# A planner for one NeuronCore: when a projection group may follow its own sum, how bursts of small matmuls are formed, and how long transfers are taken to last

## The chip, the cores and the metric

One core of one Trainium2 chip runs the whole program. The time is the device time of one execution in microseconds; the table further down has the runs of the kernel before. A profile of one more execution gives the trace from which all durations here are read.

## What is computed

One step of a decoder layer with two recurrent branches: 16 meta tokens and 2048 prompt tokens, and beside them 8 sample sequences of 4 tokens. Both branches read the same normalised input through one wide projection.

```python
h = rmsnorm(x, ln1_w)
p = h @ w_in                                  # 1024 -> 10384 columns
# branch A, 8 heads of 128: short convolution + SiLU on q, k, v, then the gated delta rule by chunks of 64
t_inv = solve(eye + lower, eye)               # lower: strict triangle of k_beta k^T * decay, per chunk and head
for chunk:                                    # the state s is carried from chunk to chunk
    v_new = u - w @ s
    o     = (q * exp(gc)) @ s + qk @ v_new
    s     = s * exp(g_last) + k_tail^T @ v_new
# branch B, 16 heads of 64: RWKV-7, S = S diag(w) - (S kk)(kk*a)^T + v k^T,  y = S r
x = x + (sig(gA) * (A @ w_out_a) + sig(gB) * (B @ w_out_b)) @ w_out
y = rmsnorm(x, lnf_w)
```

## The kernel before

**Tiles and stages.** Tokens are cut into chunks of 64, and the 33 chunks into five segments of 6 or 7 chunks, so that a tile is 128 features by 384 or 448 tokens. In each segment there are four units "G" (branch A, two heads each) and eight units "R" (branch B, two heads each). A unit first has its projections (stage P), then its preparation (stage M: norms, pairwise products, transposes, the inverse of the triangle), then its chain over the chunks (stage C), in which each chunk needs the state of the chunk ahead of it. Around them stand the projections of the gates and three output projections ("f", br 0 to 2: `w_out_a`, `w_out_b`, `w_out`).

**The projections.** `proj` sums 24 matmuls of 128x128 into one PSUM tile `ps_p`: the input is held as a high and a low part (`hHL`, or `mhl` for the last projection) and so are the weights (`wh`, `wl`). Half of a tile is 12 matmuls, 8 with `wh` and 4 with `wl`; the planner keeps them as groups of six (`PG`). Each weight half is loaded from HBM by SyncE (SP) into one of ten slots with tag `w`, and SP issues all DMAs in one order.

**The small matmuls.** The chain and the preparation work on 64x64 or 128x64 pieces. The planner calls a form of the array a mode: F is 128x128 (projections, transposes, column sums), A is up to 64 by up to 64, B 128 by up to 64, C 64 by 128. In the trace they show as `128*128`, `64*64`, `128*64` and `64*128`. In the chain of a G unit the PSUM tile is `ps_g` and the tiles are `gs` (state), `gR`, `wbd`; in that of an R unit `ps_c`, `X`, `rR`, `xo`. Each chunk visits TensorE three or four times, and between two visits VectorE or ScalarE has to turn PSUM into the next operand. Such a pair of visits is called a link below.

**The inverse.** `send_blocks` and `g_inv` write the diagonal blocks to DRAM (`ex`, eight DMAs), read them back in another layout (`iM`), invert them on VectorE (`iD`, `iT`), write them (`bk`) and read them into `Dn` and `Dt` by sixteen DMAs; then TensorE multiplies out of `Dn` into `ps_n`.

**What sets the order.** Nothing runs as it was written down: `Rec` records the operations as nodes with dependences, and `Sched.run` plays through them with costs of its own (`cost`, L346; a transfer lasts `n.lat` = 2.1, L366) and appends each node to one order when it starts. `replay` (L875 in the profile) then emits that order, so each engine gets a fixed queue, and on the chip an engine waits at the head of its queue. In `run`, a node becomes ready when all it depends on has finished by the planner's clock, TensorE's own predecessors included, with 0.18 or 0.27 behind a matmul. `pick_pe` (L812) chooses TensorE's next node: it stays in a mode while that mode has ready nodes; from F it leaves for a small mode if the next projection group `pn` isn't ready, or if enough groups have run (`s.burst` counts them) and there is a link ready, or much work. `commit` (L619) lines up projection tiles and the weight loads in `worder`; `can` (L541) lets a weight load start when a slot is free, `drop` (L586) frees it.

```python
go = pn is None or (any(chain.values()) and s.burst >= BCH) or s.burst >= BMX or (val[k] >= BVL and s.burst >= BCH)
BCH, BMX, BVL, AGE, ZUR = 4, 16, 3.0, 0.1, 0.5
```

Of the kernel before, what the change touches and what calls it, by code (L numbers as in the profile page):

```python
# [16 lines left out]
C = 64  # L17
# [229 lines left out]
class Rec:  # L247
# [98 lines left out]
    def cost(s, n, e, name, a, k, outs, ins, mode):  # L346
        f = lambda x: prod(x.shape[1:])
        if e == "PE":
            n.cols += (128 if name == "transpose" else f(a[2])) * (1 if name == "transpose" or a[1].dtype == F32R else 2)
            if name == "transpose":  # L350
                n.dur += 0.107
            elif a[1].dtype == F32R:
                n.dur += (f(a[2]) / 2.4 + 14.5) / 1000
            else:
                N = f(a[2])
                n.dur += {"A": max(54, 54 + 0.5 * (N - 64)), "B": max(56, 0.86 * N), "C": max(70, 1.05 * N), "F": max(110, 4 * N / 2.4)}[mode] / 1000
            n.lat = 0.18 if a[1].dtype == F32R else 0.27
        elif e == "SP":
            o = outs[0] if outs else a[0]
            by = prod(o.shape) * 4  # L360
            last = lambda x: x.ap[-1][1] * 4 if x.ap[-1][0] == 1 else 4
            ap = [y.ap_ if isinstance(y, V) else y for y in (a[0], a[1])]
            seg = min(last(y) for y in ap)
            nd = by / max(seg, 4)
            n.kb = max(by, nd * 256)
            n.dur, n.lat = 0.07, 2.1  # L366
        else:
            N = max(f(x) for x in outs[:1] + ins[:1]) if outs else 0
            ps = any((isinstance(x, V) and x.root.psum) for x in ins)
            if e == "DVE":  # L370
                d = N / 0.96 + 160
                if name == "scalar_tensor_tensor":
                    d += 40
                if name == "tensor_tensor_scan":
                    d = 2 * N / 0.96 + 160
            elif e == "ACT":
                d = 0.82 * N + (165 if ps else 240)
            else:
                d = {"tensor_tensor": 2.35 * N + 100, "memset": 0.6 * N + 80}.get(name, 1.1 * N + 150)
            n.dur += d / 1000  # L380
            n.lat = 0.09
        if e == "PE":
            return
# [63 lines left out]
class Sched:  # L447
# [4 lines left out]
    def __init__(s, rec, porder):  # L452
# [42 lines left out]
        for u in rec.units:  # L495
            ev = []
            for j, n in enumerate(u.nodes):
                for r in n.allocs:
                    r.left = len(r.acc)
                    r.unit = u  # L500
                    k = (r.pool, r.tag)
                    if r.psum or r.tag == "w":
                        continue
                    u.seqs.setdefault(k, []).append(r)
            last = {}
            for j, n in enumerate(u.nodes):
                for r in n.roots:
                    last[r] = j
            start = {r: j for j, n in enumerate(u.nodes) for r in n.allocs}
            for k, L in u.seqs.items():  # L510
                live = []
                for i, r in enumerate(L):
                    live.append(1 + sum(1 for q in L[:i] if last[q] >= start[r] or q.unit is not u or any(m.unit is not u for m in q.acc)))
                mx = 0
                pk = [0] * (len(L) + 1)
                for i in range(len(L) - 1, -1, -1):
                    mx = max(mx, live[i])
                    pk[i] = mx
                u.peak[k], u.idx[k], u.held[k] = pk, 0, 0
                if mx > rec.slots[k]:  # L520
                    print("PEAK", u.kind, u.seg, k[1], mx, rec.slots[k])
            u.left = len(u.nodes)
            for n in u.nodes:
                u.st.setdefault(n.stage, [0, []])
                u.st[n.stage][0] += 1
                u.st[n.stage][1].append(n)
# [14 lines left out]
    def can(s, n):  # L541
        need = {}
        for r in n.allocs:
            k = (r.pool, r.tag)
            need[k] = need.get(k, 0) + 1
        u = n.unit
        for k, c in need.items():
# [1 line left out]
            if av < 0:  # L549
                return False  # L550
            if k[1] == "w":
                if not s.worder or s.worder[0] is not n:
                    return False
                continue
            if k[0].space == PSUM:
# [30 lines left out]
    def drop(s, r):  # L586
        k = (r.pool, r.tag)
        s.free[k].append(r.slot)
        if k in r.unit.held and not r.psum and r.tag != "w":
            r.unit.held[k] -= 1  # L590

# [108 lines left out]
    def run(s):  # L700
# [2 lines left out]
        E = ["PE", "DVE", "ACT", "POOL", "SP"]  # L703
        s.rdy = {e: [] for e in E}
        s.active, s.worder, s.pq, s.cur, s.infl, s.wpend = [], [], [], None, [], []
        s.lastunit, s.late = s.porder["last"], s.porder["late"]
        tfree = dict.fromkeys(E, 0.0)
        s.mode, s.burst = "F", 0
# [3 lines left out]
        ev, c = [], 0  # L712
# [8 lines left out]
        while done < total:  # L721
            s.commit()
            prog = True
            while prog:
                prog = False
                for e in E:
# [7 lines left out]
                    if e == "PE":  # L734
# [9 lines left out]
                            s.cols[w] = s.cols.get(w, 0) + n.cols * part / d  # L744
                        s.mode = n.mode
                        isP = n.pt is not None and len(n.ops) * 2 > PG
                        s.burst = s.burst + 1 if isP else (s.burst if n.mode == "F" else 0)
                        s.stat["P" if isP else "s"] += n.dur
                        s.stat["idle"] += s.now - max(tfree[e], 0)
# [3 lines left out]
                        s.rdy[e].remove(n)  # L753
                    s.take(n)
                    n.started, n.start = True, s.now
                    s.on_started(n)
                    out.append(n)
                    nstart += 1
# [8 lines left out]
                    heapq.heappush(ev, (fin, c, n))  # L767
                    if e == "PE":
                        s.commit()
            if not ev:  # L770
                self_dump(s)
                raise RuntimeError("stuck")
# [5 lines left out]
            for n in L:  # L778
                if n is None:
                    continue  # L780
                done += 1
                n.unit.left -= 1
                if n.unit.left == 0:
                    s.active.remove(n.unit)
                for r in n.roots:
                    r.left -= 1
                    if r.left == 0:
                        s.drop(r)
                for m in n.succ:
                    m.nd -= 1  # L790
                    m.rt = s.now
                    if m.nd == 0 and m.en and not (m.pt is not None and m.eng == "PE"):
                        s.rdy[m.eng].append(m)
        s.order = out
        return out

    def clock(s):
        w = int(s.now / 3.4133)
# [13 lines left out]
    def pick_pe(s):  # L812
# [10 lines left out]
        else:  # L823
# [8 lines left out]
            T = {k: L for k, L in R.items() if k != "F"}  # L832
            if T:
                val = {k: sum(x.dur + (0.5 if x.cls == 0 else 0.0) for x in L) + AGE * max(s.now - x.rt for x in L) for k, L in T.items()}
                chain = {k: any(x.cls == 0 for x in L) for k, L in T.items()}
                k = max(T, key=lambda k: (val[k], k))
                go = pn is None or (any(chain.values()) and s.burst >= BCH) or s.burst >= BMX or (val[k] >= BVL and s.burst >= BCH)
                if go:
                    n = min(T[k], key=key)
            if n is None and "F" in R:  # L840
# [19 lines left out]
                    print("       ", r.name, "next", L[i].name, i, len(L), "free", len(s.free[k]), "peak", u.peak[k][i], [(v.age, v.held.get(k), v.peak[k][v.idx[k]] if k in v.idx else None) for v in s.active])  # L860


BCH, BMX, BVL, AGE, ZUR = 4, 16, 3.0, 0.1, 0.5


def replay(tc, rec, order):
# [1446 lines left out]
```

## Time and profile before

| what | us |
| --- | --- |
| runs | 4485.87, 4490.87, 4494.15; median 4490.87 |
| the profiled execution's own time | 4488.34 |
| its span, first to last instruction | 4486.6 |
| VectorE, ScalarE, GpSimd busy | 2725.4, 1973.8, 984.4 |
| read from HBM, written | 602.29 MB, 180.56 MB |

The profile groups instructions by source line and tile names; as `replay` emits everything, one line stands for all, and the tile names tell the work. "Idle before" is the time for which an engine had nothing running ahead of an instruction, with the instruction or DMA that ended it. Single-precision matmuls that aren't of the rounded kind stand as two records each, so a chain step of two matmuls shows as x4.

### The profile page before, as it was taken

How to read it: one execution, taken by the hardware profiler on the slowest of the kernel's cores; microseconds unless marked ns; L12 is line 12 of the kernel's file. 1: busy time of each engine (PE TensorE's matmuls, PEld its weight loads, DVE VectorE, ACT ScalarE, POOL GpSimd, SP SyncE). 2: the span in 40 equal slices, each digit the busy share in tenths (PEclk: the TensorE clock that was granted, in tenths of full speed). 3: DMA queues.
4: the chain of work that ended last, by engine and by line, in shares of the span. 5: the costliest groups of instructions: out<-in, count | busy, mean ns of one | idle time of the engine just before them, and what ended most of it. 6: DMA issues, size and time to landing. Idle time of an engine off the chain costs nothing. (4 is left out here: it accounts for less than half of the span.)

```text
span 4486.6 us, 91248 instructions
## 1 busy us (share of the span) xinstructions
PE 4138.6 (92%) x32684; PEld 3467.9 (77%) x32684; DVE 2725.4 (61%) x7052; ACT 1973.8 (44%) x4842; POOL 984.4 (22%) x1972
## 2 busy tenths in 40 slices
PE   6788999998999999998999999999999999989997
PEld 6677777777878788877777787878777888768776
DVE  5877766756666554556667544676654547656642
ACT  5444543434445344444444442545444434544431
POOL 3333333323122121112212121121122102211210
PEclk9887898899999899999999999999999999999998
DMA  7544665659645456754445576544446865444457
GB/s 253 179 139 139 194 222 173 193 192 306 189 130 164 126 175 214 248 175 121 138 125 150 166 238 212 178 127 144 135 135 183 258 192 174 137 122 131 142 181 241
DMA packets 660687, 790.08 MB, mean 176 GB/s; under 512 B 251105, under 2 KB 347209, under 8 KB 660234
## 3 DMA queue, kind: packets, MB, share of 16 engines
q1 hardware_dynamic: 660234, 784.25, 56.5%
q8 instruction: 259, 4.24, 0.4%
q14 instruction: 194, 1.59, 0.1%
HBM read 602.29 MB, written 180.56 MB: 174 GB/s over the span
## 5 line engine op out<-in xcount | busy, mean ns | idle before, releaser
L875 PE MATMUL ps_p<-hHL,wh 128*128 128x448 f32 (+3 forms) x7760 | 1938.3, 378 | 39.2 <-DMA wh<-wh 20.3
L875 PEld LDWEIGHTS ps_p<-hHL,wh 128*128 128x128 f32 x7760 | 1395.4, 195 | 186.6 <-issue 62.7
L875 PE MATMUL ps_p<-hHL,wl 128*128 128x448 f32 (+3 forms) x3880 | 910.1, 357 | 1.5 <-DVE wl L875 1.0
L875 PEld LDWEIGHTS ps_p<-hHL,wl 128*128 128x128 f32 x3880 | 727.8, 193 | 36.8 <-DVE wl L875 1.6
L875 POOL COPY xo<-X 64x64 f32<-64x64 f32 x528 | 177.4, 336 | 819.5 <-ACT X L875 445.2
L875 DVE TENSOR_TENSOR iT<-iM,iD 56x1 f32<-56x1 f32 (+1 forms) x900 | 293.2, 326 | 72.4 <-DMA iD<-in_consts 54.7
L875 ACT COPY raw<-ps_p 128x448 f32<-128x448 f32 (+3 forms) x285 | 144.0, 505 | 341.2 <-PE ps_p L875 316.2
L875 DVE SCALAR_TENSOR_TENSOR cv<-raw,pv,cv 128x448 f32<-128x448 f32 (+1 forms) x360 | 261.1, 725 | 37.0 <-ACT cv L875 28.1
L875 DVE TENSOR_REDUCE iD<-iT 56x1 f32<-56x1 f32 (+1 forms) x900 | 205.1, 228 | 17.6
L875 POOL TENSOR_TENSOR wl<-wr,wh 128x512 fp32r<-128x512 f32 x105 | 146.4, 1394 | 218.7 <-ACT wh L875 101.9
L875 ACT ACTIVATE X<-ps_c,dc 64x64 f32<-64x64 f32 x224 | 69.0, 309 | 266.7 <-DVE X L875 153.4
L875 ACT CAST wh<-wr 128x512 fp32r<-128x512 f32 x210 | 129.3, 616 | 114.5 <-PE ps_p L875 36.2
L875 ACT ACTIVATE X<-ps_c 64x64 f32<-64x64 f32 x264 | 54.3, 216 | 261.7 <-DVE X L875 134.9
L875 DVE SCALAR_TENSOR_TENSOR gs<-gs,gl,ps_g 128x128 f32<-128x128 f32 x264 | 84.5, 344 | 125.2 <-PE ps_g L875 86.8
L875 POOL TENSOR_TENSOR Nt<-AL,consts 64x448 f32<-64x448 f32 (+1 forms) x80 | 93.7, 1171 | 292.9 <-DVE AL L875 288.4
L875 PE MATMUL ps_p<-mhl,wh 128*128 128x448 f32 (+2 forms) x640 | 156.1, 371 | 0.6 <-DMA wh<-wh 0.4
L875 ACT ACTIVATE sig<-cv 128x448 f32<-128x448 f32 (+2 forms) x120 | 67.4, 561 | 185.6 <-DVE cv L875 184.3
L875 PE MATMUL ps_g<-gs,cv 128*64 128x128 f32 x1056 | 122.1, 307 | 25.7 <-DVE wbd L875 9.6
L875 DVE TENSOR_SCALAR X<-ps_c,dc 64x64 f32<-64x64 f32 x224 | 65.1, 291 | 128.2 <-PE ps_c L875 83.8
L875 PEld LDWEIGHTS ps_n<-Z,Wp 64*64 64x64 f32 x3168 | 113.2, 146 | 34.5 <-DVE Z L875 15.4
L875 PE MATMUL ps_n<-Z,Wp 64*64 64x16 f32 (+1 forms) x3168 | 123.1, 222 | 12.4 <-DVE Z L875 12.1
L875 DVE TENSOR_TENSOR Z<-Dt,ps_n 128x336 f32<-128x336 f32 (+1 forms) x180 | 67.0, 372 | 101.7 <-PE ps_n L875 84.2
(337 smaller groups left out, 7483.4 us busy)
## 6 DMA issues: line engine op xcount, KB each, us to landing
wh<-wh SPq DMA_DIRECT2D x1050, 256.0 KB
wl<-wl SPq DMA_DIRECT2D x1050, 256.0 KB
wr<-in_wt SPq DMA_DIRECT2D x210, 256.0 KB
gl<-gt SPq DMA_DIRECT2D x72, 224.0 KB
gt<-gt SPq DMA_DIRECT2D x48, 224.0 KB
xt<-in_x_prompt SPq DMA_DIRECT2D x29, 256.0 KB
xt<-in_x_prompt SPq DMA_DIRECT2D x13, 512.0 KB
out_y_p<-xt SPq DMA_DIRECT2D x26, 256.0 KB
```

The source lines that it names most:

```text
L875: getattr(getattr(nc, eng), name)(*[g(x) for x in a], **{q: g(x) for q, x in k.items()})
```

## The change

Six edits, all in the planner; no operation is added or left out, and both orders have 23653 matmuls.

1. A node of TensorE that depends on another node of TensorE counts that one as done when it starts (`settle`, called at the start), not when it ends plus 0.18 or 0.27. A group that goes on with its own sum, and any other matmul behind TensorE's own work, may go at once.
2. Leaving F for a link: it is no longer enough that one unit's link is ready and four groups have run. There must be links of as many units as have a chain begun and unfinished (`na`), or one that has been ready for 3.0 (`TWAIT`).
3. Out of a small mode, the next small mode with ready nodes is taken, not the projections (`DIR`).
4. `BCH`, `BMX`, `BVL` go from 4, 16, 3.0 to 2, 8, 1.5.
5. Transfers other than weight loads are taken to last 3.0 in place of 2.1 (`DLAT`).
6. A weight slot is not reused for 1.0 after it was freed (`WMAR`), by the planner's clock.

```diff
-            n.dur, n.lat = 0.07, 2.1
+            n.dur, n.lat = 0.07, WLAT if n.stage == "W" else DLAT
...
+            k = sum(1 for n in u.nodes if n.eng == "PE" and n.stage == "C" and n.mode in "AB")
+            u.chain = [k, k]
...
-                if not s.worder or s.worder[0] is not n:
+                if not s.worder or s.worder[0] is not n or (WMAR and s.freed.get(s.free[k][0], 0) > s.now - WMAR):
...
+                    if e == "PE":
+                        for m in n.succ:
+                            if m.eng == e:
+                                s.settle(m)
...
                 for m in n.succ:
-                    m.nd -= 1
-                    m.rt = s.now
-                    if m.nd == 0 and m.en and not (m.pt is not None and m.eng == "PE"):
-                        s.rdy[m.eng].append(m)
+                    if m.eng != n.eng or m.eng != "PE":
+                        s.settle(m)
...
-                chain = {k: any(x.cls == 0 for x in L) for k, L in T.items()}
+                na = sum(1 for u in s.infl if 0 < u.chain[0] < u.chain[1])
+                chain = {}
+                for k, L in T.items():
+                    C = [x for x in L if x.cls == 0]
+                    chain[k] = bool(C) and (len({x.unit for x in C}) >= na or max(s.now - x.rt for x in C) >= TWAIT)
...
-                go = pn is None or (any(chain.values()) and s.burst >= BCH) or s.burst >= BMX or (val[k] >= BVL and s.burst >= BCH)
+                go = pn is None or (s.mode != "F" and val[k] >= DIR) or (any(chain.values()) and s.burst >= BCH) or s.burst >= BMX or (val[k] >= BVL and s.burst >= BCH)
...
-BCH, BMX, BVL, AGE, ZUR = 4, 16, 3.0, 0.1, 0.5
+BCH, BMX, BVL, AGE, ZUR = 2, 8, 1.5, 0.1, 0.5
+WLAT, DLAT, WMAR = 2.1, 3.0, 1.0
+DIR = 0.0
+TWAIT = 3.0
```

Two places show what becomes of TensorE's order. The first is the end of the chain of the last R unit, in the last segment: the column sums over `sh` and `sl` (high and low part) are its last visits to TensorE, and behind them stand the projections. Before:

```order
L875 MATMUL ps_p<-hHL,wh 128x448 x2
L875 MATMUL ps_p<-hHL,wl 128x448 x4
L875 MATMUL ps_a<-consts,rs_277 64x64 x2
L875 MATMUL ps_p<-hHL,wh 128x448 x6
L875 MATMUL ps_n<-sh,bocm 128x448
L875 MATMUL ps_n<-sl,bocm 128x448
L875 MATMUL ps_p<-hHL,wh 128x448 x2
L875 MATMUL ps_p<-hHL,wl 128x448 x4
L875 MATMUL ps_a<-sh,bocm 128x448
L875 MATMUL ps_a<-sl,bocm 128x448
L875 MATMUL ps_p<-hHL,wh 128x448 x8
```

The same place of the order now:

```order
L903 MATMUL ps_p<-hHL,wh 128x448 x8
L903 MATMUL ps_p<-hHL,wl 128x448 x4
L903 MATMUL ps_n<-sh,bocm 128x448
L903 MATMUL ps_n<-sl,bocm 128x448
L903 MATMUL ps_a<-consts,rs_277 64x64 x2
L903 MATMUL ps_p<-hHL,wh 128x448 x8
L903 MATMUL ps_p<-hHL,wl 128x448 x4
L903 MATMUL ps_a<-sh,bocm 128x448
L903 MATMUL ps_a<-sl,bocm 128x448
L903 MATMUL ps_p<-hHL,wh 128x448 x8
```

Twelve projection matmuls now stand between two visits of the chain where six stood. Of the projections behind the last row of `sl`, up to the first that reads `mhl`, there were 192, which are the eight tiles of the second output projection; now there are 324, so 132 matmuls of earlier work have moved behind the chain's end and ahead of the first matmul that needs its result.

The second place is a G unit in the fourth segment, where TensorE first multiplies out of `Dn`, with the chains of another G unit (`ps_g`) and an R unit (`ps_c`) around it. Before:

```order
L875 MATMUL ps_p<-hHL,wh 128x448 x2
L875 MATMUL ps_p<-hHL,wl 128x448 x4
L875 MATMUL ps_p<-hHL,wh 128x448 x6
L875 MATMUL ps_g<-gR,Z 64x128 x2
L875 MATMUL ps_c<-rR,Z 64x64 x2
L875 MATMUL ps_n<-Dn,Nt 64x64 x14
L875 MATMUL ps_p<-hHL,wh 128x448 x2
L875 MATMUL ps_p<-hHL,wl 128x448 x4
```

The same unit in the order now:

```order
L903 MATMUL ps_p<-hHL,wh 128x448 x6
L903 MATMUL ps_g<-gR,Z 64x128 x2
L903 MATMUL ps_n<-Dn,Nt 64x64 x14
L903 MATMUL ps_c<-X,AL 64x64 x2
L903 MATMUL ps_g<-gs_264,cv 64x128
L903 MATMUL ps_g<-wbd_259,KE 64x128
L903 MATMUL ps_g<-gs_265,cv 64x128
L903 MATMUL ps_g<-wbd_259,KE 64x128
L903 MATMUL ps_g<-wbd_259,ktl 128x256
L903 MATMUL ps_p<-hHL,wh 128x448 x2
```

The burst now goes from the 64x64 form straight to the 128x64 form and holds the next step of both chains; between `gR,Z` and the step behind it on the same unit there is no projection matmul any more. And between this unit's pairwise product and `Dn` there are now 140 projection matmuls where there were 96.

More of the change, by code (lines that the diff above doesn't have):

```diff
@@ L588, in drop @@
         s.free[k].append(r.slot)
+        if r.tag == "w":
+            s.freed[r.slot] = s.now
+            if WMAR:
+                s.wake.append(s.now + WMAR + 0.001)
         if k in r.unit.held and not r.psum and r.tag != "w":
@@ L705, in run @@
         s.active, s.worder, s.pq, s.cur, s.infl, s.wpend = [], [], [], None, [], []
+        s.freed, s.wake = {}, []
         s.lastunit, s.late = s.porder["last"], s.porder["late"]
@@ L746, in run @@
                         isP = n.pt is not None and len(n.ops) * 2 > PG
+                        if n.stage == "C" and n.mode in "AB":
+                            n.unit.chain[0] -= 1
                         s.burst = s.burst + 1 if isP else (s.burst if n.mode == "F" else 0)
@@ L769, in run @@
                         s.commit()
+            for x in s.wake:
+                c += 1
+                heapq.heappush(ev, (x, c, None))
+            s.wake = []
             if not ev:
@@ L789, in run, with settle @@
                 for m in n.succ:
-                    m.nd -= 1
-                    m.rt = s.now
-                    if m.nd == 0 and m.en and not (m.pt is not None and m.eng == "PE"):
-                        s.rdy[m.eng].append(m)
+                    if m.eng != n.eng or m.eng != "PE":
+                        s.settle(m)
         s.order = out
         return out
+    def settle(s, m):
+        m.nd -= 1
+        m.rt = s.now
+        if m.nd == 0 and m.en and not (m.pt is not None and m.eng == "PE"):
+            s.rdy[m.eng].append(m)
     def clock(s):
```

## The prediction

> **What bounds the kernel now.** I read the page first, then the clock, then the waits of TensorE, then stretches of its timeline.
>
> ```profile
> span 4486.6 us, 91248 instructions
> ...
> PE 4138.6 (92%) x32684; PEld 3467.9 (77%) x32684; DVE 2725.4 (61%) x7052; ACT 1973.8 (44%) x4842; POOL 984.4 (22%) x1972
> ```
>
> TensorE is busy for 92% and no other engine for over 61%, so the kernel is bound by TensorE. But "busy" holds three things that are no work: the time lost when the array changes its form, the time at half clock, and, in the other 8%, waits. The planner can touch only these three, since both orders hold the same 23653 matmuls.
>
> ```profile
> core 0: 4486.6 us, clock 0.936
> ```
>
> The clock row gives the second: single stretches of the timeline run at full or at half speed, so a mean of 0.936 says that 2 x 6.4% = 13% of the span, some 574 us, ran at half. By stretches, the first 1000 us are much worse than the rest:
>
> ```profile
> 0.00:1000.00 1000.00, 874.32 (x6912) 725.65 (x6913) 691.54 (x1865) 459.06 (x1142) 325.71 (x620) 0.86 0.59 187
> 1000.00:4487.00 3487.00, 3264.23 (x25774) 2742.22 (x25772) 2033.82 (x5187) 1514.78 (x3701) 658.66 (x1352) 0.96 0.56 173
> ```
>
> The third is in the table of who waited for whom (us in total, times, longest):
>
> ```profile
> PE ps_c L875 <- DVE X L875: 39.6, 28, 6.5
> PE ps_n L875 <- DMA Dn<-bk: 34.1, 23, 5.7
> PE ps_p L875 <- DMA wh<-wh: 20.7, 4, 16.6
> ...
> PE ps_c L875 <- DVE rR L875: 16.7, 17, 4.0
> PE ps_g L875 <- DVE gR L875: 16.3, 16, 5.4
> PE ps_c L875 <- ACT X L875: 15.1, 17, 3.0
> ...
> PE ps_n L875 <- DMA Dt<-bk: 7.3, 5, 2.6
> ```
>
> The waits are many and short; the largest single one is 16.6 us. The rows of `X`, `rR` and `gR` are links of the chains (87.7 us in 78 waits, 1.12 each), those of `Dn` and `Dt` the inverse's way through DRAM.
>
> **Term 1, changes of form.** What does a visit to a small form cost? First a stretch of projections without any, then one visit, then one change inside a burst:
>
> ```profile
> 3504.43 1.76 PE L875 MATMUL ps_p<-hHL,wh 128*128 128x448 f32 x8
> 3506.03 0.96 PE L875 MATMUL ps_p<-hHL,wl 128*128 128x448 f32 x4
> 3506.83 1.76 PE L875 MATMUL ps_p<-hHL,wh 128*128 128x448 f32 x8
> ```
>
> ```profile
> 4358.59 1.48 PE L875 MATMUL ps_p<-hHL,wh 128*128 128x448 f32 x6
> 4360.00 0.33 PE L875 MATMUL ps_c<-rR,Z 64*64 64x64 f32 x4
> 4360.26 0.68 PE L875 MATMUL ps_p<-hHL,wh 128*128 128x448 f32 x2
> ```
>
> ```profile
> 3280.33 0.34 PE L875 MATMUL ps_c<-RH,xo 128*64 128x64 f32 x4
> 3280.45 0.34 PE L875 MATMUL ps_c<-AY,X 128*64 128x64 f32 x4
> 3280.71 0.99 PE L875 MATMUL ps_n<-Z,Wp 64*64 64x16 f32 x28
> ```
>
> Twelve projection matmuls take 3506.83 - 3504.43 = 2.40 us, 0.20 each. Four small records take 3280.45 - 3280.33 = 0.12. Both starting points of the visit stand just behind a return: 4360.26 - 4358.59 = 1.67, less 6 x 0.20 and less 0.12, leaves 0.35 us for leaving and coming back. Inside a burst the change costs 3280.71 - 3280.45 - 0.12 = 0.14.
>
> Counted by the forms of the matmuls, the order of before leaves the 128x128 form 1196 times, the new one 893 times; changes among small forms go from 258 to 647 (2650 and 2433 changes in all). So 303 visits fewer x 0.35 = -106 and 389 changes more x 0.14 = +54: **-52 us**. Upper end: nothing, since a visit from a transpose rather than a projection may be cheaper than the one I priced; lower end -106, if changes inside a burst hide behind each other.
>
> The Trainium skill, page "TensorEngine Tiling (Array Packing)", section "Key Properties", says that a change of the tiling mode drains TensorE, and speaks of no cheaper change between two small modes, which is against going from mode to mode. By it each change costs alike, half a visit, and the term would be 217 x 0.175 = -38. The rows have 0.14 against 0.175, so the rule is nearly right and the sum barely moves.
>
> **Term 2, the end of the last chain.** The wait of 16.6 us stands at the first place of the order shown above, and the chain of waits says what it was made of:
>
> ```profile
> 4376.16 0.47 PE L875 MATMUL ps_a<-sl,bocm 128*128 128x448 f32 x1 [0.93 <-DVE sl L875]
> 4393.25 3.33 PE L875 MATMUL ps_p<-hHL,wh 128*128 128x448 f32 x8 [16.61 <-DMA wh<-wh]
> ```
>
> ```profile
> 4380.55 0.38 SPq L875
> ...
> 4383.44 4.94 DMA hHL<-oB
> 4388.39 4.72 DMA wh<-wh
> ```
>
> The last unit's result is stored at about 4380, SP issues the eight loads of it into `hHL`, and behind them, in SP's queue, the weights. Now 132 matmuls x 0.20 = 26.4 us of projections stand behind the chain's end, which covers the 4 us to the store, and in SP's new order the weights of five halves stand ahead of the loads. What is late next: the loads overwrite the tiles that the first output projection reads, so they start only when its last tile is nearly done. A load takes 4.94, I allow 1 for its split into high and low part, and four of the eight may start some 3 us early. I take 5 us of wait as left (ends 0 and 16.6): **-12 us**.
>
> **Term 3, Dn and Dt.** The rows above hold 41.4 us. The planner counted an issue on SP as 0.07; SP needs
>
> ```profile
> L875 SPq DMA_DIRECT2D Dn<-bk x480: 302/427/1750, 161.5 to 4290.7; - x160
> ```
>
> so the eight loads of `Dn` and eight of `Dt` come 16 x 0.36 = 5.7 us later than planned, and `DLAT` gives back 0.9 in each of four transfers in a row, 3.6. Eight of the 60 units account for most of these waits. In their orders, the projection matmuls between pairwise product and `Dn` go from 140, 126, 138, 156, 132, 138, 96 and 126 to 196, 168, 162, 182, 184, 144, 140 and 184: 38 more on average, 7.7 us, against a longest wait of 5.7. Over all 60 the median goes from 132 to 147. I take three quarters of the 41.4: **-30 us** (ends 0, if SP's queue makes the loads later by as much, and -41).
>
> **Term 4, links.** I put the waits of the chains into classes by how many projection matmuls the order has between the two visits. Before, of 162 links with none, 66 waited, 0.29 us per link over all 162; of 468 with up to six, 0.115; of 286 with seven to twelve, 0.026; of 220 with more, 0.021. The new order has 281, 25, 633 and 197 of them: 81 + 3 + 17 + 4 = 105 against 113 us. **-7 us**. The two parts pull against each other: twelve matmuls between links in place of six cover nearly every link, but bursts that hold two steps of one chain make 119 more links without cover. Ends: -50, if the 119 stand behind other small work, as `gR,Z` does behind 14 matmuls of `Dn` in the order; +126 is the slower rival's.
>
> **Term 5, the clock behind a wait.** A wait costs more than itself. At the second place of the order:
>
> ```profile
> 3028.57 0.44 PE L875 MATMUL ps_n<-Dn,Nt 64*64 64x64 f32 x2 [2.32 <-DMA Dn<-bk]
> 3030.18 1.75 PE L875 MATMUL ps_n<-Dn,Nt 64*64 64x64 f32 x26 [1.16 <-DMA Dn<-bk]
> 3031.86 1.11 PE L875 MATMUL ps_p<-hHL,wh 128*128 128x448 f32 x2
> 3032.77 1.70 PE L875 MATMUL ps_p<-hHL,wl 128*128 128x448 f32 x4
> 3034.40 0.70 PE L875 MATMUL ps_g<-gs,cv 128*64 128x128 f32 x4
> ...
> 1988.65 1.00 PE L875 MATMUL ps_n<-Dn,Nt 64*64 64x64 f32 x26 [1.21 <-DMA Dn<-bk]
> 1989.58 0.67 PE L875 MATMUL ps_p<-hHL,wh 128*128 128x448 f32 x2
> ```
>
> The 26 records take 3031.86 - 3030.18 = 1.68 against 0.93 at full clock, the six projections behind them 2.54 against 1.20: 2.1 us on top of the 3.5 us waited. Eight such units: **-17 us** (ends 0 and -34).
>
> How long must a wait be for this? Here one of 2.35 us was enough, six projections taking 2.20 behind it (up to the next start) and 1.13 ahead of it:
>
> ```profile
> 1602.76 1.20 PE L875 MATMUL ps_p<-hHL,wh 128*128 128x384 f32 x6
> 1603.89 0.34 PE L875 MATMUL ps_c<-X,AL 128*64 128x64 f32 x4
> ...
> 1607.83 0.74 PE L875 MATMUL ps_a<-consts,xt 128*128 128x128 f32 x4 [2.35 <-issue]
> 1608.21 2.27 PE L875 MATMUL ps_p<-hHL,wh 128*128 128x384 f32 x6
> 1610.41 0.48 PE L875 MATMUL ps_c<-rR,Z 64*64 64x64 f32 x4
> ```
>
> The Trainium skill, page "TensorE: Matmul & The Clock Gate", section "HAM oscillation — how this bites in real kernels", has the abstract rule that idle gaps over about 3.4 us must be avoided. By it most of the waits here, which are shorter, would cost no clock, and term 5 would fall away; this trace disagrees, with its 2.35 us.
>
> **What costs nothing, I hold.** The later reuse of a weight slot (`WMAR`) delays loads by up to 1.0 by the planner's clock; what hides it is that weights come early: besides the 16.6 us, the row `wh` above holds three waits of 4.1 us in all. If that cover went, I would expect those to double, +4. Longer bursts could by themselves lack the matmul columns that keep the clock up; the bursts that hold over 2.5 us of work by the rows' durations go from 20 to 50, but none of the trace's half-clock rows that I read began without a wait, so I count 0.
>
> Not seen by any of this is where the new order meets the chip badly: each order has its own spots where the plan was too hopeful, and I removed only those of the old one. I add back a third of terms 2, 3 and 5: **+20 us**.
>
> **Sum.** 4488.34 (the profiled execution) - 52 - 12 - 30 - 7 - 17 + 20 = 4390. The median of the runs lies 2.5 us above the profiled execution, so 4393.
>
> **Rivals.**
> - *The waits only move.* For: the Dn waits are a plan's error of some us, and such errors are as likely in a new order; terms 2 to 5 give nothing. Against: 38 more matmuls ahead of `Dn`, and 132 behind the last chain. Only the changes of form stay: 4488 - 52 + 2.5 = 4439.
> - *Short waits cost no clock*, as the rule on the gate would have it. Then removing waits under 3.4 us brings only themselves: 4393 + 17 = 4410. The 2.35 us row speaks against it.
> - *Waits fall everywhere.* Edit 1 makes the plan truer, and with `DLAT` all 41 us of Dn and Dt go, half of the links' 113, and in the first 1000 us the clock rises from 0.86 half way to 0.96, 50 us: 4488 - 52 - 17 - 41 - 56 - 17 - 50 + 2.5 = 4258; with half of the excess over my sum, 4325.
> - *Slower: bursts become the place to wait.* The 119 more links without cover each wait the mean of the chain rows, 1.12 us: +133; every fourth also loses the clock, 30 x 2.1 = +63. In place of -7 that gives 4393 + 7 + 196 = 4596. For: uncovered links had the dearest class. Against: only 66 of 162 waited. It decides from (98 - 7 + 9) / 119 = 0.84 us per link, where the time would be slower by 0.2%.
> - *Within 0.2%*, about what a measurement of this kernel can tell from no change: the links take back just what the rest gives, 0.7 to 0.8 us each. That the change does nothing is excluded by the order.
>
> **Chances.** Forecast 0.50; waits only move 0.18; waits fall everywhere 0.13; short waits cost no clock 0.04; within 0.2% 0.06; slower 0.09. Faster by over 0.2%: 0.50 + 0.18 + 0.13 + 0.04 = 0.85. The range goes from 4315, which takes in most of the wide gain, to 4465, which takes in the moved waits.
>
> **What would show it.** Right: TensorE's busy time falls by some 50 to 70 us; the row `Dn<-bk` under 12 us and `Dt` near 0; at the end one wait of about 5 us on `hHL` in place of 16.6; clock about 0.945; rows of `X`, `rR` and `gR` together near 80. Wrong: a clock at or under 0.936, rows of `ps_c` and `ps_g` that hold over 200 us (the slower rival), or a `Dn` row as long as before (SP's queue). If busy time falls by 50 and idle time not at all, the waits have moved.

## The result, and the profile after

| | before | now |
| --- | --- | --- |
| median of the runs, us | 4488.37 (4482.38 to 4494.15, 4 runs) | **4363.57** (4352.51 to 4371.86, 4 runs) |
| ratio, with its 95% interval | | 0.9721 (0.9695 to 0.9746) |
| the profiled execution, and its span | 4488.34; 4486.6 | 4371.86; 4370.1 |

The kernel is 125 us faster. The forecast was 4393, so the gain came out 29 us larger than its sum. The first lines of the profile's page for the changed kernel, and its clock row:

```profile
span 4370.1 us, 91290 instructions
...
PE 4066.9 (93%) x32684; PEld 3485.0 (80%) x32684; DVE 2726.3 (62%) x7052; ACT 1965.2 (45%) x4842; POOL 992.3 (23%) x1972
```

```profile
core 0: 4370.1 us, clock 0.941
```

TensorE is busy for 4138.6 - 4066.9 = 71.7 us less with the same number of matmuls, and idle for 348.0 - 303.2 = 44.8 us less. The other engines do what they did. The two stretches of the prediction again (their columns: length, busy time and count of PE, PEld, DVE, ACT, POOL, then PE's clock, the DMA share and GB/s):

```profile
0.00:1000.00 1000.00, 867.00 (x6959) 730.75 (x6960) 707.13 (x1872) 466.93 (x1151) 333.29 (x624) 0.86 0.59 189
1000.00:4371.00 3371.00, 3199.92 (x25726) 2754.28 (x25725) 2019.17 (x5181) 1498.31 (x3691) 659.01 (x1348) 0.96 0.58 178
```

The first 1000 us run at 0.86 as before, and hold only 47 more of the 32684 records; nearly all of the gain lies behind them. Who TensorE waited for, in the rows that answer to those of before (us in total, times, longest):

```profile
PE ps_c L903 <- DVE X L903: 26.9, 22, 4.3
PE ps_c L903 <- DVE rR L903: 26.0, 20, 5.2
...
PE ps_g L903 <- DVE gR L903: 11.4, 5, 5.1
PE ps_c L903 <- ACT X L903: 10.7, 20, 1.4
...
PE ps_n L903 <- DMA Dt<-bk: 8.4, 6, 2.6
...
PE ps_n L903 <- DMA Dn<-bk: 4.5, 7, 1.1
...
PE ps_p L903 <- DMA wh<-wh: 2.0, 2, 1.0
```

`Dn` and `Dt` fell from 41.4 to 12.9 us. All rows of `ps_c` and `ps_g`, the chains, fell from 121.9 to 97.4. The 16.6 us on `wh` are gone. All waits of the table together went from 331.4 to 289.4 (without the row of `ps_a` that names no releaser, 2.4 us before).

To see where the span went, the same sum was made over the trace of every kernel: from each matmul record's start to the next start, less the median distance of that kind behind its own kind at full clock. What is over goes into three heaps: under 0.7 us at full clock (changes of form, above all), 0.7 us or more at any clock (stalls), and under 0.7 us at a lower clock.

| us | span | forms | stalls | half clock |
| --- | --- | --- | --- | --- |
| before | 4486.6 | 393 | 295 | 233 |
| now | 4370.1 | 321 | 266 | 204 |
| difference | -116.5 | -73 | -29 | -29 |

What is left, +15 us, is in the medians themselves and at both ends.

The heaps are an estimate. The heap of forms also holds waits of under 0.7 us, and its size hangs on what is taken as a kind: with kinds by both tile names and shape it falls from 586 to 532, with kinds by PSUM tile and shape from 514 to 443. (With kinds by shape alone, which mix different work, it rises from 475 to 526, as the medians themselves shift.) Stalls and half clock fall in the first two recounts as well, by 35 and by 25 to 32.

### The profile page after: what moved, and what is told of

It reads as the page before. It is cut to its first block, busy times and chain, and to the rows that moved or that the text cites. A ratio compares the mean times of both kernels' runs of the same rounds, so it can differ in the third digit from the quotient of the medians.

```text
span 4370.1 us, 91290 instructions
## 1 busy us (share of the span) xinstructions
PE 4066.9 (93%) x32684; PEld 3485.0 (80%) x32684; DVE 2726.3 (62%) x7052; ACT 1965.2 (45%) x4842; POOL 992.3 (23%) x1972
## 5 line engine op out<-in xcount | busy, mean ns | idle before, releaser
L903 PE MATMUL ps_p<-hHL,wh 128*128 128x448 f32 (+3 forms) x7760 | 1828.1, 373 | 30.7 <-ACT wh L903 10.3
L903 PEld LDWEIGHTS ps_p<-hHL,wh 128*128 128x128 f32 x7760 | 1421.3, 195 | 156.1 <-issue 28.3
L903 PE MATMUL ps_p<-mhl,wh 128*128 128x448 f32 (+2 forms) x640 | 141.5, 359 | 5.7 <-ACT wh L903 4.5
L903 DVE TENSOR_SCALAR X<-ps_c 64x64 f32<-64x64 f32 x264 | 58.8, 227 | 131.1 <-PE ps_c L903 88.9
L903 PE MATMUL ps_a<-RH,LH 64*128 64x128 f32 x1056 | 129.3, 292 | 0.0
```

What stands on the lines that cost most here:

```text
L903: getattr(getattr(nc, eng), name)(*[g(x) for x in a], **{q: g(x) for q, x in k.items()})
```

## The experiments

Twelve kernels ran. In some expectations, and below, visits are the leavings of the 128x128 form in the planner's own order, counted by its nodes: 1139 before and 839 now, with 253 and 639 changes inside bursts (the prediction's 1196 and 893 count the finished program by matmuls). "Links" are the chain's, by the projection matmuls between two visits: none, up to 6, up to 12, more. Ratios are to the kernel before as it ran beside each (medians of 4488 to 4494), with 95% intervals; the clock, and the waits of TensorE for `Dn` and `Dt` and in its chain rows (`ps_c`, `ps_g`), are from one profiled execution each.

| run | what differs | median, us | ratio | clock | Dn, Dt | chains |
| --- | --- | --- | --- | --- | --- | --- |
| before | | 4488.37 | 1 | 0.936 | 41.4 | 121.9 |
| now | all six edits | 4363.57 | 0.9721 (0.9695 to 0.9746) | 0.941 | 12.9 | 97.4 |
| e1 | without edit 1 | 4425.83 | 0.9851 (0.9826 to 0.9875) | 0.952 | 32.7 | 102.9 |
| e2 | without edit 5 | 4339.99 | 0.9661 (0.9647 to 0.9675) | 0.949 | 17.6 | 104.5 |
| e3 | now, reshuffled | 4344.03 | 0.9673 (0.965 to 0.9697) | 0.943 | 7.9 | 104.1 |
| e4 | before, reshuffled | 4523.91 | 1.0078 (1.0058 to 1.0097) | 0.934 | 45.4 | 134.1 |
| e5 | before, edit 1 alone | 4880.23 | 1.0877 (1.084 to 1.0915) | 0.872 | 47.7 | 272.3 |
| e6 | without edit 4 | 4546.79 | 1.0131 (1.01 to 1.0161) | 0.915 | 18.1 | 190.5 |
| e7 | before, transfers 3.2 | 4429.75 | 0.9871 (0.9842 to 0.99) | 0.945 | 13.7 | 115.6 |
| e8 | now, SP's issue 0.42 | 4246.63 | 0.9468 (0.9439 to 0.9497) | 0.957 | 2.6 | 86.4 |
| e9 | before, SP's issue 0.42 | 4298.55 | 0.9576 (0.9544 to 0.9608) | 0.956 | 13.2 | 52.1 |
| e10 | e8, reshuffled | 4236.65 | 0.9443 (0.9408 to 0.9477) | 0.958 | 4.1 | 67.4 |
| e11 | without edit 3 | 4505.05 | 1.0032 (1.001 to 1.0055) | 0.924 | 6.2 | 148.2 |
| e12 | edit 6 nearly undone | 4323.78 | 0.9633 (0.9596 to 0.9671) | 0.952 | 11.4 | 101.1 |

### How much is the luck of an order? (e3, e4)

`AGE` weighs the age of a waiting node by a tenth; 0.11 changes ties and near-ties all over the program and no rule. e3 is the changed kernel with it, e4 the kernel before.

```diff
-BCH, BMX, BVL, AGE, ZUR = 2, 8, 1.5, 0.1, 0.5
+BCH, BMX, BVL, AGE, ZUR = 2, 8, 1.5, 0.11, 0.5
```

> A control: the changed planner with AGE at 0.11 in place of 0.10, which has no meaning for the chip but gives another order (855 visits, 649 inside; 287, 22, 666 and 161 links with none, up to six, up to twelve and more projection matmuls as cover). Theory: 16 visits and 10 changes more are 7 us: 4371, and what any new order moves by chance is under 20 us. Rival (the gain of the change is a lucky order): over 30 us away from 4364, towards 4488.

> The same control on the kernel before: AGE at 0.11 (1154 visits, 247 inside, before 1139 and 253). Theory: 5 us more by changes of form, 4490 within 20. Rival (an unlucky order before): over 30 us below 4488.

A reshuffle without meaning moved the one by -20 and the other by +36 us. e3 came out 27 below its 4371 and e4 34 above its 4490, both more than the 20 that the theory allowed, and neither as its rival has it. So no edit that moves the time by less than some 35 us can be judged by its time alone; with two reshuffles this is a rough size. And the gain itself is no luck of the order: 4344 against 4524 is more than 4364 against 4488. The wait at the end of the last chain, which term 2 counted as removed, came back in e3:

```profile
PE ps_p L903 <- DMA wh<-wh: 21.4, 5, 16.6
```

It has its 16.6 us with all six edits in force, and its order has 192 projection matmuls behind the chain's end, as before, not 324. That the wait is gone in the changed kernel is luck of the order.

### Edit 1, taken out and put in alone (e1, e5)

e1 is the changed kernel in which a node again counts as done for TensorE only at its planned end:

```diff
-                    if e == "PE":
-                        for m in n.succ:
-                            if m.eng == e:
-                                s.settle(m)
...
-                    if m.eng != n.eng or m.eng != "PE":
-                        s.settle(m)
+                    s.settle(m)
```

> The changed planner without its first edit: a matmul node that depends on TensorE's own work counts it as done when it ends plus 0.18 or 0.27, as before; all other edits stay. Its order leaves the 128x128 form for a small one 1075 times (before 1139, changed 839, counted by the same tally) and changes 536 times between small forms (253, 639). Theory (changes of form carry the gain, 0.35 us a visit and 0.14 us inside a burst): 236 visits more x 0.35 less 103 x 0.14 is 68 us more than the changed kernel, 4430, and some 20 us more for links, since 548 of them have six projection matmuls as cover: 4430 to 4450. Rival (the longer transfers and the weight margin carry it, edits 5 and 6): within 15 us of the changed kernel, 4350 to 4380.

Measured 4425.83: 62 us over the changed kernel, 4 us below what the theory said. The forms heap is 418 us in place of 321, so the saving in forms hangs on edit 1. The clock is higher without it, 0.952, so in this pair part of the saving is paid back there: (1 - 0.952) x 4421.4 = 212 us were lost to it, against 258 in the changed kernel. And the wait for `Dn` is back, with transfers still counted as 3.0:

```profile
PE ps_n L898 <- DMA Dn<-bk: 24.8, 20, 4.0
...
PE ps_n L898 <- DMA Dt<-bk: 7.9, 11, 1.6
```

e5 is the reverse: the kernel before with these same lines the other way round, and nothing else.

> The kernel before with the first edit alone (a matmul node may follow TensorE's own work at once), thresholds and all else as before. Its order changes form least of all so far: 695 visits to small forms and 657 changes among them (before 1139 and 253). But 764 links of the chains have no projection matmul as cover (before 162, changed 281). From the runs so far a visit is worth 0.5 us, a change inside 0.2, a link without cover 0.25 to 0.29. Theory (edit 1 only pays together with the smaller thresholds of edit 4, because bursts of 16 groups starve the chains): -222 + 81 for forms, +100 for links, and some 80 for the clock behind those waits: 4490 + 40 = 4530, not under 4450. Rival (edit 1 alone carries the gain): 4490 - 141 = 4350.

Slower was right, but 390 us in place of some 40. The page of e5, its clock row, and the largest of its waits:

```profile
PE 4284.3 (87%) x32684; PEld 3650.5 (75%) x32684; DVE 2745.2 (56%) x7052; ACT 1980.5 (40%) x4842; POOL 988.6 (20%) x1972
```

```profile
core 0: 4898.7 us, clock 0.872
```

```profile
PE ps_c L883 <- ACT X L883: 82.3, 104, 7.3
```

Its order leaves 128x128 only 695 times and has the smallest forms heap of all, 265 us. But of its 1136 links 764 have no projection between them, and they waited 0.35 us each. The chain rows hold 272.3 us, and what the clock lacks of full speed went from 6.4% to 12.8%. Fewer changes of form, bought with uncovered links, is the slower rival of the prediction in full.

### Edits 4 and 3, taken out (e6, e11)

e6 has the old thresholds:

```diff
-BCH, BMX, BVL, AGE, ZUR = 2, 8, 1.5, 0.1, 0.5
+BCH, BMX, BVL, AGE, ZUR = 4, 16, 3.0, 0.1, 0.5
```

> The changed planner with its fourth edit undone: BCH, BMX, BVL at 4, 16, 3.0 again. 611 visits, 796 changes inside (changed 839, 639); 666 links without cover (281). Theory (smaller thresholds keep the chains moving): forms -114 + 31, links +92, clock behind them +74: 4364 + 83 = 4447, and the wait rows of ps_c and ps_g go from 97 to near 190 us. Rival (only changes of form count): 4364 - 83 = 4280.

The theory's mechanism holds: 666 uncovered links at 0.28 us, and chain rows of 190.5 us as expected. The time was 100 us above its number. For the clock behind the waits it had counted 74 us; (1 - 0.915) x 4550.5 = 387 against 258 is 129. For forms it had counted -83; in the first two recounts the heap of forms falls by 36 and 25 only.

e11 takes out the rule that goes from one small mode to the next:

```diff
-DIR = 0.0
+DIR = 1e9
```

> The changed kernel without edit 3: out of a small mode the planner may go back to the projections. Its order leaves 128x128 975 times in place of 839, has 396 changes among small forms in place of 639, and 390 links without cover in place of 281. Theory (a visit costs 0.35, a change inside 0.14, an uncovered link 0.25): +48 - 34 + 27 = +41, so 4405, 4380 to 4430 with the luck of the order; the chain rows near 125 us. Rival (going from mode to mode brings nothing, as visits and changes trade evenly): 4345 to 4375, chain rows near 97.

4505.05, 141 us above the changed kernel and 0.3% slower than the one before. The direction is the theory's, the size again not: 390 links without cover cost 0.30 each, and the chain rows hold 148.2 in place of the expected 125.

```profile
PE ps_c L903 <- ACT X L903: 43.2, 49, 5.2
```

```profile
core 0: 4520.1 us, clock 0.924
```

The clock is most of what the theory left out. The time lost at half speed is what the clock lacks of full speed times the span: (1 - 0.941) x 4370.1 = 258 us in the changed kernel, (1 - 0.924) x 4520.1 = 344 here, 86 more. The profiled execution is 17 us above the median, though; at 0.931, the median clock of the ten runs, it is some 53 more.

### Edits 5 and 6, taken out (e2, e12)

```diff
-WLAT, DLAT, WMAR = 2.1, 3.0, 1.0
+WLAT, DLAT, WMAR = 2.1, 2.1, 1.0
```

> The changed planner with its fifth edit undone: transfers last 2.1 again. Changes of form stay (836 visits, 635 inside). The projection matmuls between pairwise product and Dn fall from a median of 147 back to 132, and 15 units have under 120 (changed 7, before 18). Theory: the waits for Dn and Dt come back to 30 to 40 us from 12.9 and bring 10 to 17 us at half clock: 4364 + 27 + 14 = 4405. Rival (Dn was covered by the larger bursts, not by the counted length): rows of Dn and Dt under 20 us, time 4355 to 4375.

The theory fell. With transfers counted as 2.1 again the time is 24 us lower, within the luck of the order, and these are its rows:

```profile
PE ps_n L903 <- DMA Dn<-bk: 12.4, 15, 2.0
...
PE ps_n L903 <- DMA Dt<-bk: 5.2, 5, 1.5
```

17.6 us, not 30 to 40. So in the new order it isn't `DLAT` that keeps `Dn` from being late. What `DLAT` does show on is VectorE, whose wait for `iM`, the step ahead of `Dn`, is 105.1 us in e2 against 69.8 in the changed kernel and 135.3 before.

e12 counts the margin for a freed weight slot as 0.1:

```diff
-WLAT, DLAT, WMAR = 2.1, 3.0, 1.0
+WLAT, DLAT, WMAR = 2.1, 3.0, 0.1
```

> The changed kernel with edit 6 nearly undone: a weight slot may be used again 0.1 after it was freed, in place of 1.0. Its order has 842 visits and 620 changes inside (839 and 639). Theory (the later reuse is hidden, weights come early): no more than the luck of the order, 4335 to 4390, and waits on wh within 10 us of the 10 to 20 of the changed kernel. Rival (the margin protects against weights that come late): waits on wh of over 40 us and 4400 or more.

4323.78 is 11 us below what the theory allowed for, and waits on `wh` are 0.9 us against 2.0. (The expectation's "10 to 20" for `wh` was misread from the rows: 14.7 us stand there for weights that ScalarE makes, 2.0 for the load.) The margin protects against nothing that can be seen; whether it costs some of those 40 us, or the order was lucky, is not settled.

### Longer transfers in the old planner (e7)

```diff
-            n.dur, n.lat = 0.07, 2.1
+            n.dur, n.lat = 0.07, 2.1 if n.stage == "W" else 3.2
```

> The kernel before with transfers other than weights counted as 3.2 in place of 2.1 and nothing else (3.0 alone ends in a plan that gets stuck). Forms as before (1167 visits, 244 inside). Projection matmuls between pairwise product and Dn: median 148, 11 units under 120 (before 132 and 18; changed 147 and 7). Theory as predicted (the cover in matmuls decides): rows of Dn and Dt fall from 41 to under 20 us, time 4490 - 21 - 12 = 4457. Rival (pace: as long as the planner puts 0.18 us between the groups of a sum that the chip doesn't need, projections on the chip run ahead of the plan and every transfer comes late): rows of Dn and Dt stay at 30 or more, time within 30 us of 4490.

By itself, edit 5's idea is worth 59 us on the old planner and takes `Dn` and `Dt` from 41.4 to 13.7. With a visit count of 1167 the forms stay (406 us), as they should. In the changed kernel it brings nothing of that, as e2 shows.

### What an issue on SyncE costs (e8, e9, e10)

The planner counts a DMA's issue as 0.07 us of SP's time. Here is a place of the kernel before that the prediction's Dn rows come from, SP's queue first, then VectorE, then TensorE (start, duration; what ended the idle time ahead in brackets):

```profile
3025.22 3.73 SPq L875 DMA_DIRECT2D Dn<-bk  x8
3029.00 3.73 SPq L875 DMA_DIRECT2D Dt<-bk  x8
3032.77 0.42 SPq L875 DMA_DIRECT2D iD<-in_consts  x1
3033.29 0.34 SPq L875 DMA_DIRECT2D wh<-wh  x1
3033.72 0.38 SPq L875 DMA_DIRECT2D wl<-wl  x1
3034.15 0.41 SPq L875 DMA_DIRECT2D iM<-ex  x1
```

```profile
3026.40 0.22 DVE L875 TENSOR_SCALAR X<-ps_c 64x64 f32<-64x64 f32 x1
3037.03 0.29 DVE L875 TENSOR_SCALAR iM<-iM 56x256 f32<-56x256 f32 x1 [10.41 <-DMA iM<-ex]
...
3037.54 0.29 DVE L875 TENSOR_SCALAR X<-ps_c,dc 64x64 f32<-64x64 f32 x1
...
3038.04 0.35 DVE L875 SCALAR_TENSOR_TENSOR gs<-gs,gl,ps_g 128x128 f32<-128x128 f32 x1
```

```profile
3039.12 0.44 PE L875 MATMUL ps_g<-gs,cv 128*64 128x128 f32 x4 [1.45 <-DVE gs L875]
```

The sixteen loads of `Dn` and `Dt` keep SP busy from 3025.22 to 3032.77, 7.55 us where the plan has 16 x 0.07 = 1.1. Behind them stands another unit's `iM`. VectorE has it at the head of its queue and stands still for 10.41 us, and behind it stand the next `X` and `gs` of two chains; TensorE then waits 1.45 us for `gs`. So a load that nobody on TensorE waits for holds up the chains. e8 is the changed kernel, e9 the kernel before, with a count that agrees with these rows:

```diff
-            n.dur, n.lat = 0.07, 2.1
+            n.dur, n.lat = 0.42, 2.1
```

> The changed planner with SP's issue of a transfer counted as 0.42 in place of 0.07, near the 0.43 that the trace has for the loads of Dn. 866 visits, 639 inside; 312 links without cover; Dn median 168, 4 units under 120. Theory (VectorE's waits for iM and TensorE's for Dn are off the path by now): VectorE's wait for iM falls from 70 to under 40 us, Dn and Dt under 8, but the time moves by less than 20 us from 4364, +14 for forms and +8 for links. Rival (late transfers still hold the chains up through VectorE's queue): 4320 or less.

> The kernel before, with nothing changed but the planner's count of a DMA issue on SyncE (0.42 in place of 0.07). Its order leaves 128x128 about as often as before (1163 and 1154 to 1167 in the two other variants of the old planner), so forms bring nothing. Theory: the price of the issue works by itself, through VectorE's queue: VectorE's wait for iM falls from 135 to 20 to 40 us, Dn and Dt from 41 to under 10, the first 1000 us rise from a clock of 0.86 to about 0.91, and the time is 4350 to 4400, at least 30 below the 4430 that longer transfers alone gave. Rival (the price only pays where bursts hold several chains, since only there a stalled VectorE holds more than one of them): iM and Dn fall, but the time stays at 4420 to 4460.

> The changed kernel with the issue on SyncE counted as 0.42, as in the run of 4247, and AGE 0.11 in place of 0.1, which only reshuffles the order. Theory (late transfers were the cause of the gain): 4220 to 4280, iM under 40 us, Dn and Dt together under 8. Rival (the 4247 was a lucky order): back towards 4340, with a clock near 0.943.

For e8 my theory was wrong by 100 us and the rival right: 4246.63. Its rows fell as the theory had them (VectorE's wait for `iM` to 21.4 us, `Dn` and `Dt` to 2.6), but they were not off the path. The reshuffled e10, 4236.65, shows that it wasn't luck. And e9, **one number in the old planner, gives 4298.55**, 65 us faster than the six edits under study. Its clock, TensorE's waits, and VectorE's for `iM` in e9 and, below it, in the kernel before:

```profile
core 0: 4296.0 us, clock 0.956
```

```profile
PE ps_c L875 <- DVE rR L875: 12.7, 16, 1.6
...
PE ps_n L875 <- DMA Dn<-bk: 9.8, 12, 2.3
...
PE ps_c L875 <- DVE X L875: 8.3, 17, 1.5
PE ps_c L875 <- ACT X L875: 8.2, 19, 1.0
```

```profile
DVE iM L875 <- DMA iM<-ex: 52.5, 28, 5.1
```

```profile
DVE iM L875 <- DMA iM<-ex: 135.3, 46, 10.4
```

The rows of `X` and `rR` hold 29.2 us where they held 39.6 + 16.7 + 15.1 = 71.4, and `iM` 52.5 where it held 135.3. In three numbers the expectation was too hopeful (`iM` 20 to 40, `Dn` and `Dt` under 10, a clock of 0.91 in the first 1000 us, where it is 0.89), and the time came out below its range all the same. What longer transfers (e7) don't do and this does is seen in the waits of all feeding engines for DMAs (VectorE, ScalarE, GpSimd, added over the rows of each), and in TensorE's for VectorE:

| us | for DMAs: VectorE | ScalarE | GpSimd | TensorE for VectorE |
| --- | --- | --- | --- | --- |
| before | 277 | 181 | 370 | 195 |
| e4 | 281 | 173 | 325 | 189 |
| now | 227 | 154 | 369 | 196 |
| e3 | 185 | 129 | 364 | 151 |
| e7 | 197 | 117 | 386 | 167 |
| e9 | 134 | 109 | 242 | 119 |
| e8 | 61 | 98 | 220 | 120 |
| e10 | 74 | 107 | 147 | 100 |

A flat 3.2 is the same for a load at an empty queue and for the sixteenth of a row of loads, which stands behind 15 x 0.47 = 7.1 us of other issues in the rows above; a count per issue follows the queue. That this is why e9 gains more than e7 is argued from the table, and no run separates it. In the order under study TensorE's waits for VectorE stayed at 196 us, but its reshuffle e3 has 151, so that is a matter of the order. The Trainium skill, page "Perfetto Trace Analysis", section "What "DMA-bound" means", lists an issuing engine's sequencer track that is solid with DMA slices as a bound of its own, since those slices are descriptor generation and not data movement. The rows of SP above agree for their stretch: 7.55 us without a gap of more than 0.05.

With the issue counted rightly the six edits are still worth something, 4298.55 - 4246.63 = 52 us, or 62 with e10. In the three heaps that is:

| us | span | forms | stalls | half clock |
| --- | --- | --- | --- | --- |
| e9 | 4296.0 | 423 | 162 | 150 |
| e8 | 4241.8 | 342 | 181 | 138 |
| e10 | 4237.0 | 350 | 168 | 129 |

Forms fall by 73 to 81 and half clock by 12 to 21; stalls don't fall. e9 itself was not reshuffled, and in the old planner a reshuffle alone moved the time by 36, so 52 to 62 is not far above luck.

## Why the prediction was right, and where not

That the change is faster, and by changes of form, waits and clock together, is what the runs show. That the time came within 29 us of the forecast is in part luck: a reshuffle alone moves it by -20 to +36. Most of the signs that I had named came: TensorE's busy time 71.7 us lower (50 to 70 expected), a clock of 0.941 (0.945), rows of `X`, `rR` and `gR` of 75 us (80), and 3.6 us of waits on `hHL` (5) in place of 16.6.

**Forms (-52): right in kind, between -42 and -73.** The heap gives -73, but it also holds short waits. Busy time fell by 71.7 us, and at most 29 of that is the clock, which leaves 42. That orders with fewer visits lose less to forms is beyond luck: the five orders with 1075 to 1167 visits (before, e1, e4, e7, e9) hold 393 to 423 us, the six with 836 to 873 (now, e2, e3, e8, e10, e12) hold 321 to 350, and the two sets stay apart in the first two recounts. The price of a change inside a burst is not settled. If the 303 visits fewer are worth 0.35 each and all 73 us are forms, the 389 changes inside come to (106 - 73) / 389 = 0.085 and not to the 0.14 that I read from a single burst. By e1, whose heap is 25 us above that of before with 64 visits fewer and 283 changes more, they come to (25 + 22) / 283 = 0.17. The Trainium skill's rule on a drain at each change of mode (page "TensorEngine Tiling (Array Packing)", section "Key Properties") has no price; with one price for all, half a visit, the term would have been -38. Between 0.085 and 0.17 these runs don't decide for or against it.

What I missed is what this saving rests on. I counted the finished order and didn't ask which edits it hangs on. Edit 1 alone costs 390 us (e5), and the whole without edit 3 or without edit 4 costs 141 (e11) and 183 us (e6) more than with it, so that nothing of the gain is left. Edit 1 makes longer runs of projections and of small work; edits 3 and 4 keep the chains fed while it does (281 links without cover with all edits, 390 without edit 3, 666 without edit 4). Edit 2 was not taken out by itself.

**The end of the last chain (-12): the number right, its reading as a property of the change wrong.** 5 us were to be left; the loads of `hHL` left these:

```profile
4273.95 0.47 PE L903 MATMUL ps_p<-hHL,wh 128*128 128x448 f32 x1 [2.87 <-ACT hHL L903]
4274.61 0.68 PE L903 MATMUL ps_p<-hHL,wh 128*128 128x448 f32 x2 [0.19 <-DVE hHL L903]
4275.86 2.24 PE L903 MATMUL ps_p<-hHL,wh 128*128 128x448 f32 x5 [0.57 <-POOL hHL L903]
```

That is 3.6 us, and the chain of waits has the steps I named:

```profile
4268.37 4.88 DMA hHL<-oB
...
4273.33 0.56 ACT hHL L903
```

The cover decides, as I had it: all ten orders with 192 projection matmuls there (before, e3 to e11) have a wait of 16.4 to 17.3 us on `wh`, and the four with 276 to 384 (now, e1, e2, e12) don't. But e3, e6, e8, e10 and e11 all have edit 1 and most of the others. The 132 matmuls behind the chain's end belong to single orders, not to the rules.

**Dn and Dt (-30): the size right, -28.5, the step that gave its cause wrong.** The reshuffled kernels (e3: 7.9, e4: 45.4) say that the fall is no luck. I laid it to `DLAT` and to more projection matmuls ahead of `Dn`. `DLAT` taken out gives back 4.7 us (e2), edit 1 taken out 19.8 (e1). And the count of matmuls doesn't order the waits: over the 60 units its median is 132 before and in e2, 142 in e1 and 144 in e11, and the waits are 41.4, 17.6, 32.7 and 6.2. What edit 1 does for these waits is not settled. Of the rows that I had named as signs, `Dn` under 12 was right, `Dt` near 0 was not (8.4, from 7.3).

**Links (-7): -18 by the same count.** By classes the waits fell from 113 to 95 us in place of 105. Links without cover cost 0.25 each in place of 0.29, 71 us in all, and those with 7 to 12 matmuls what I took, 0.029. The short cover of six, 53.6 us before, had probably been dear because VectorE was late: in e9, with 476 such links, they waited 12.4 us.

**Clock (-17): about -29**, by the heap and by (1 - clock) x span (287 to 258). Waits of around 2 us do count. For each fall of the clock in the trace I took the longest TensorE wait that reaches into the 3.4 us ahead of it. Of the 65 falls before, 56 have one of over 0.7 us; the median is 1.8, and it is over 3.4 us in 16. Of the 60 now these are 54, 2.5 and 22. The rival by the Trainium skill's 3.4 us (page "TensorE: Matmul & The Clock Gate", section "HAM oscillation — how this bites in real kernels") lets this term fall away; these rows speak against it, with 49 of 65 falls and 38 of 60 that have no wait so long. The 0 that I counted for long bursts is not quite right: nine falls before have no wait of over 0.7 us, and in five of these nine TensorE spent 89 to 100% of the 3.4 us ahead on small forms, against 27% over the whole trace. But now there are six such falls, so this moved little.

**The +20 for new bad spots: right in size, 24.** TensorE's waits in the rows that belong to no term rose from 331.4 - 41.4 - 121.9 - 16.6 = 151.5 to 289.4 - 12.9 - 97.4 - 3.6 = 175.5, among them those of `ps_a` (83.3 to 90.4) and of `ps_n` other than `Dn` and `Dt` (29.6 to 33.7).

**The 29 us by which the time fell short of the forecast.** The measures above overlap and don't add up; three that do are these. Idle time fell by 44.8, where terms 2 to 4 and the +20 make -29. The clock gave 29 in place of 17. The rest of busy time gave 42 in place of 52, if all that the clock cost lies in busy time. Together that is the span's 116.5 against 98, 18 us more. The other 11 are no term at all: the profiled execution was the slowest of its four and lies 8.3 us above the median, where I had put the median 2.5 above it.

**The rivals.** "The waits only move" (4439) is out: TensorE is idle for 44.8 us less. "Waits fall everywhere" (4325) is out, the first 1000 us stand at 0.86. "Slower" is out here and came true in e5, e6 and e11, at 0.28 to 0.35 us for an uncovered link, not at the 0.84 that I had taken as its threshold: with 390 to 764 links without cover in place of 281 it decides at a far lower price for each, and the clock falls with them. None of my rivals spoke of the largest thing in this kernel, SP's queue holding VectorE, though the 0.07 stood in my text: I used it for the sixteen loads of one unit, and not for who stands behind them.

## What to carry to other kernels

Give a planner the measured cost of every resource that works in a queue before tuning its rules: here one number for a DMA's issue (0.07 to 0.42) was worth 190 us on the old rules, in one order, six edits of rules 125, and both together 242 to 252 (ratios 0.9468 and 0.9443). Look for the load that stands ahead of other work in a feeding engine's queue, even when the bounding engine never waits for that load itself. And before crediting an edit, run a reshuffle that means nothing: here it moved the time by up to 36 us, and of rules that depend on each other two, taken out one at a time, cost more than all six had brought.

## What was not expected of the hardware

The clock answers to many short waits: e5, whose longest chain wait is 7.3 us, lost 0.128 x 4898.7 = 627 us to it, 340 more than before, while all its waits grew by 263 (331.4 to 594.7). Of its 92 falls, 73 have no wait of over 3.4 us reaching into the 3.4 us ahead. A few falls in the kernel before stand behind a stretch of small forms with no wait of over 0.7 us (the paragraph on the clock). Whether a change between two small forms costs less than half of leaving and coming back is not shown: the two estimates above, 0.085 and 0.17 us, lie on either side of the 0.14 of the single burst, and half a visit is 0.175.
